# First network of a diffusion layer: 14 of 22 weight pairs as seven products of block sums, gated rows kept in DRAM

## Chip, cores, metric

One NeuronCore of one Trainium2 chip runs one launch of the kernel. The metric is device time in microseconds (us), the median over runs. The engines are called PE (TensorE), DVE (VectorE), ACT (ScalarE), POOL (GpSimd) and SP (SyncE, which here only issues DMAs). Every operand is float32 or float32r.

## What is computed

One layer of a hybrid diffusion backbone, on 512 latent tokens and 256 context tokens of width 1024. The part that changes is the first half-step feed-forward network, which runs on both token kinds with the same weights and with modulation vectors of their own:

```python
def swiglu(u, w_up, w_down):
    a, b = jnp.split(u @ w_up, 2, axis=-1)
    return (jax.nn.silu(a) * b) @ w_down          # w_up 1024 x 5632, w_down 2816 x 1024

def ffn_sublayer(h, m, i, w_up, w_down):
    shift, scale, gate = sub_mod(m, i)            # three of nine vectors, silu(c) @ w_ada + b_ada
    y = swiglu(modulate(h, shift, scale), w_up, w_down)
    return post_ln(DEEPNORM_ALPHA * h + 0.5 * gate * y, ln_g[i], ln_b[i])

x = ffn_sublayer(x, mod_x, 0, ffn1_w_in, ffn1_w_out)
ctx = ffn_sublayer(ctx, mod_c, 0, ffn1_w_in, ffn1_w_out)
```

After it come the input projections, neighbourhood attention and gated DeltaNet, their merge, and a second feed-forward network on the latent tokens alone. These do not change.

## The kernel before

**Accuracy.** Every float32 operand of the large products is split in a high and a low half (`split`, lines 134 to 139: ACT casts to float32r, DVE subtracts), and each 128 x 128 block is multiplied three times: high x high, low tokens x high weights, high tokens x low weights (lines 192 to 194 for the up-projections, line 211 for the down-projections).

**Tiling.** The 5632 columns of `w_up` are 22 pairs of 128 gate and 128 value columns. One pair is two weight tiles of 128 x 1024 (eight blocks along the 1024 inputs). `ffn_unit` multiplies a pair with all 512 latent or all 256 context tokens into two PSUM banks, and `glu` gates the result (silu on ACT, product on DVE) and splits it into `hx` (latent) or `hc` (context).

**Order.** (1) Pairs 0 to 2 on latent tokens while the modulation of the tokens is still being made; pairs 3 to 7 on latent tokens, with the context's modulation between; then pairs 0 to 7 on context tokens, their weights loaded again. (2) `up_phase`: pairs 8 to 10, each on both kinds. (3) `down` for the first 11 rows of `w_down`: all four latent blocks of 128 tokens in eight PSUM banks, then both context blocks. The results are gated, added to the inputs and kept in SBUF as `accx` and `accc` (lines 481 and 482). (4) `up_phase` for pairs 11 to 21. (5) `down` for the other 11 rows, then normalisation (`finish1`), and transposing and splitting of the new tokens (`u2`).

**What runs beside it.** The other modulation vectors are made on DVE. `ada_gen` is a generator; each step loads one 128 x 1024 tile of the transposed `w_ada` and takes its dot product with one or two broadcast rows (`dot_cols`, line 281). There are 56 steps, the first 24 with two dots. `up_phase` takes four steps per pair.

**What sets the order.** Weights go through `Stream`: loads on the SP queue, a raw buffer, then the split, one tile ahead of use and limited by the buffers (two high/low buffers in `wp`, every third tile in the one of `wx`). Raw buffers for weights, modulation tiles and token rows come from one counter, `raw1()`, which goes round five buffers: two in `wp`, two in the pool `more[0]` and one in `wx`. The program is traced in the order of its text; the framework's scheduler then fixes each engine's and queue's order ahead of time by a timing model of its own, adds the semaphores and hands out buffers. At run time each queue keeps to that order.

The second network already runs most of its pairs as seven products (lines 1456 to 1521), with token halves of 256.

Of the kernel before, what the change touches and what calls it, by code (L numbers as in the profile page):

```python
# [18 lines left out]
P = 128  # L19
# [39 lines left out]
def body(ctx, tc, I, out, dbg=None):  # L59
# [223 lines left out]
    def load_crow(tp):  # L283
        r = tl(tp, [P, 2, D], "crow")
        nc.scalar.dma_start(r[0:1], I["c_row"])
        return r

# [8 lines left out]
    def ada_gen(tp, wp, crow):  # L296
        for sec in range(2, 9):
            which = [(0, colx)] + ([(1, colc)] if sec < 5 else [])
            sl = slice(sec * 8, sec * 8 + 8)
            for k in range(KT):  # L300
                raw = raw1()
                nc.sync.dma_start(raw[:], I["w_adaT"][sec * KT + k])
                for w, col in which:
                    dot_cols(tp, raw, crow[:, w], col, sec * 8 + k)
                if k < KT - 1:
                    yield
            for w, col in which:
# [12 lines left out]
    raws, more = [0], [None]  # L320
# [6 lines left out]
    ap_, close_ap = pool("acc1")  # L327
    hcp, close_hcp = pool("hc1")
    up, close_up = pool("u1")

    uxh = tl(up, [P, KT, NX], "uxh", 1, F32R)
    uxl = tl(up, [P, KT, NX], "uxl", 1, F32R)

    tl(up, [P, 16], "gap")
    uch = tl(up, [P, KT, NCT], "uch", 1, F32R)
    ucl = tl(up, [P, KT, NCT], "ucl", 1, F32R)
    tl(up, [P, 48], "gap2")
# [7 lines left out]
    hxp, close_hxp = pool("hx1", "right")  # L345
    tp, close_tp = pool("t1")
    more[0] = tp
    xn = {"x": [], "c": []}

    def modulate_k(pp, kind, k):  # L350

        w, col, uh, ul, n = (0, colx, uxh, uxl, NX) if kind == "x" else (1, colc, uch, ucl, NCT)
# [4 lines left out]
        for sec in range(2):  # L357
            c0 = sec * 8 + k
            V.scalar_tensor_tensor(col[:, c0:c0 + 1], col[:, c0:c0 + 1], float(sec), bcol[:, c0:c0 + 1], op0=ALU.add, op1=ALU.add)
# [3 lines left out]
        u32 = tl(tp, [P, NX], "fs", 2)  # L363
        S.activation(u32[:, 0:n], ps[:], AF.Identity, bias=col[:, k:k + 1], scale=col[:, 8 + k:9 + k])
        split(u32[:, 0:n], uh[:, k], ul[:, k])

    def order1():
        t = lambda fs: [I["up1"][2 * f + j] for f in fs for j in range(2)]
        dn = lambda a, b: rows(I["dn1"], range(a, b))
        o = t(range(F0, F1)) + t(range(F1)) + t(range(F1, HF)) + dn(0, HF) + dn(0, HF - 2)  # L370
        o += t(range(HF, NF)) + dn(HF, NF - 4)
        n = len(o)
        o += dn(HF, NF - KL1)
        o = [(w, "x") if j % 3 == 2 else w for j, w in enumerate(o)]
        return o[:n] + [(w, "tail") for w in dn(NF - 4, NF)] + o[n:]

    def h_x():
        h = tl(hxp, [P, 2, NX], "hx", HF, F32R)
        return h[:, 0], h[:, 1]

    def h_c():
        h = tl(hcp, [P, 2, NCT], "hc", HF, F32R)
# [3 lines left out]
    F0, F1, KC, KL1, KL2 = 3, 8, 2, 6, 6  # L386
    PSB = [2]
    pp0, close_pp0 = pool("pp0", space=PSUM)
    crow = load_crow(tp)
    for t in range(4):  # L390
        x_t = tl(ap_, [P, D], f"ax{t}")
        (nc.scalar if t % 2 else nc.sync).dma_start(x_t[:], tok_src("x", t))
# [3 lines left out]
    for x_t in xn["x"]:  # L396
        ln_norm(tp, x_t[:], x_t, act=True)
    nc.sync.dma_start(bcol[:], I["b_col"])
    w0, acc0 = [], []

    def start_f(f):
        for j in range(2):
            raw = tl(ap_, [P, D], f"ac{j}")
            nc.sync.dma_start(raw[:], I["up1"][2 * f + j])
            if 2 * f + j < 3:
                hi, lo = [(tl(wp, [P, D], n, WB, F32R) if 2 * f + j < 2 else tl(wx, [P, D], n, 1, F32R))[:] for n in ("wh", "wl")]
            else:
                hi, lo = [tl(hxp, [P, 2, NX], "hx", HF, F32R)[:].rearrange("p a n -> p (a n)") for _ in range(2)]
            split(raw[:], hi, lo)
# [27 lines left out]
    for t in range(2):  # L437
        raw = raw1()
        nc.sync.dma_start(raw[:], tok_src("c", t))
        xn["c"].append(tl(ap_, [P, D], f"ac{t}"))  # L440
# [1264 lines left out]
```

## Time and profile before

| | us |
|---|---|
| median of 3 runs | 1522.52 (1520.34 to 1522.91) |
| profiled execution, whole time | 1518.13 |
| its span | 1516.4 |
| PE busy | 1458.7 (96%) |
| DVE busy | 1047.0 (69%) |
| ACT busy | 607.6 (40%) |
| POOL busy | 196.4 (13%) |

The first network fills roughly the first 580 us of the span. Its stages, in us from the start of the span: latent part of pairs 0 to 7 until 119.6, context part of these pairs until 165.0, pairs 8 to 10 until 214.6, first down stage until 303.6, pairs 11 to 21 until 486.0, second down stage until about 579.5. "Busy" is the time in which an instruction runs. Matmuls are pipelined, so the distance between the starts of two of them, and not the duration in a row, is what one costs. In a row of a timeline the first number is the start, the second the duration; in a group of instructions the numbers behind the bar are the sum of busy time and the mean in ns, then the idle time before them and what ended it.

### The profile page before, as it was taken

The page shows a single profiled execution, that of the slowest core. Times are in us where ns is not written, and L with a number is a line of the kernel's source. Part 1 is how long each engine was busy: PE and PEld are TensorE (multiplying, and loading weights), DVE is VectorE, ACT ScalarE, POOL GpSimd, SP SyncE. Part 2 cuts the span into 40 slices and gives each one's busy share as a digit, 9 for nine tenths or more (in the row PEclk, how much of TensorE's full clock was granted, in tenths as well). Part 3 has the DMA queues.
Part 4 walks back from the last instruction along what each step waited for, and adds up shares of the span by engine and source line. Part 5 has one row for each costly group of instructions (what it writes and reads, how often), then busy time and mean ns, then how long its engine had stood idle before and what let it go on. Part 6 is the DMA issues. An engine that isn't in the chain of part 4 may idle for free.

```text
span 1516.4 us, 23760 instructions
## 1 busy us (share of the span) xinstructions
PE 1458.7 (96%) x9286; PEld 1259.4 (83%) x9286; DVE 1047.0 (69%) x1792; ACT 607.6 (40%) x1009; POOL 196.4 (13%) x225
## 2 busy tenths in 40 slices
PE   6999999999999999999996899999999999999997
PEld 4789988888888888889874788867778999998886
DVE  8765852597554487758777896567669699886326
ACT  5444321222222255655542444267516444444310
POOL 0000000000000011323301001243221022220001
PEclk9999999999999999999998999999999999999999
DMA  9665642667554424222476634274343143233322
GB/s 369 204 237 188 221 145 97 206 206 253 196 179 139 142 111 142 96 83 89 139 212 178 172 97 132 78 255 151 97 171 141 57 139 111 98 112 141 137 84 84
DMA packets 107587, 230.73 MB, mean 152 GB/s; under 512 B 34177, under 2 KB 47825, under 8 KB 107473
## 3 DMA queue, kind: packets, MB, share of 16 engines
q1 hardware_dynamic: 105312, 221.79, 43.5%
q10 hardware_dynamic: 1586, 5.32, 0.9%
q0 software_dynamic: 576, 2.10, 0.4%
q8 instruction: 73, 1.20, 0.3%
q14 instruction: 40, 0.33, 0.1%
HBM read 206.33 MB, written 22.85 MB: 151 GB/s over the span
## 4 chain that ended last, share of the span: by engine, by line
PE 81%; DVE 9%; DMA 5%; issue 2%; ACT 1%; POOL 1%; SPq 1%; DVEq 0%; POOLq 0%; ACTq 0%
PE ps L211 22%; PE ps L192 9%; PE ps L194 9%; PE ps L193 8%; PE pm L192 5%; PE pm L194 5%; PE pm L193 5%; PE pc L862 3%; PE ps L1492 2%; PE ps L1493 2%; PE ps L1494 2%; DVE wl L139 2%; PE po L1272 1%; DMA Dt<-gcd 1%; PE pt L1261 1%
## 5 line engine op out<-in xcount | busy, mean ns | idle before, releaser
L139 DVE TENSOR_TENSOR wl<-wr,wh 128x1024 fp32r<-128x1024 f32 (+1 forms) x215 | 263.2, 1228 | 190.3 <-ACT wh L137 189.4
L137 ACT CAST wh<-wr 128x1024 fp32r<-128x1024 f32 (+1 forms) x215 | 217.9, 1018 | 325.0 <-PE ps L211 100.8
L194 PE MATMUL ps<-uxh,wl 128*128 128x512 f32 (+1 forms) x496 | 179.7, 364 | 0.5 <-DVE wl L139 0.5
L192 PE MATMUL ps<-uxh,wh 128*128 128x512 f32 (+1 forms) x496 | 180.0, 366 | 0.0
L193 PE MATMUL ps<-uxl,wh 128*128 128x512 f32 (+1 forms) x496 | 179.5, 363 | 0.0
L281 DVE SCALAR_TENSOR_TENSOR adap<-wr,crow 128x1024 f32<-128x1024 f32 x112 | 136.8, 1222 | 39.0 <-DMA wr<-in_w_adaT_dram 37.6
L114 POOL TENSOR_TENSOR rs<-ve,mhalf 128x1 f32<-128x1 f32 (+2 forms) x46 | 50.6, 1103 | 743.4 <-DVE ve L110 740.5
L192 PE MATMUL pm<-uxh,wh 128*128 128x512 f32 x320 | 131.8, 412 | 0.8 <-ACT spill L611 0.8
L194 PE MATMUL pm<-uxh,wl 128*128 128x512 f32 x320 | 127.2, 398 | 0.7 <-DVE wl L139 0.7
L193 PE MATMUL pm<-uxl,wh 128*128 128x512 f32 x320 | 126.9, 397 | 0.0
L194 PEld LDWEIGHTS ps<-uxh,wl 128*128 128x128 f32 x496 | 93.9, 189 | 16.2 <-DVE wl L139 1.3
L192 PEld LDWEIGHTS ps<-uxh,wh 128*128 128x128 f32 x496 | 93.7, 190 | 14.6 <-issue 0.8
L193 PEld LDWEIGHTS ps<-uxl,wh 128*128 128x128 f32 x496 | 94.0, 189 | 13.9
L192 PE MATMUL ps<-uch,wh 128*128 128x256 f32 x352 | 98.6, 280 | 0.0
L194 PE MATMUL ps<-uch,wl 128*128 128x256 f32 x352 | 98.3, 279 | 0.0
L193 PE MATMUL ps<-ucl,wh 128*128 128x256 f32 x352 | 98.2, 279 | 0.0
L211 PE MATMUL ps<-wh,hx 128*128 128x512 f32 x352 | 94.8, 389 | 0.0
L211 PEld LDWEIGHTS ps<-wh,hx 128*128 128x128 f32 x352 | 65.9, 188 | 13.6
L194 PEld LDWEIGHTS pm<-uxh,wl 128*128 128x128 f32 x320 | 60.9, 190 | 14.4 <-DVE wl L139 1.5
L192 PEld LDWEIGHTS pm<-uxh,wh 128*128 128x128 f32 x320 | 61.0, 190 | 12.6 <-ACT spill L611 1.5
L193 PEld LDWEIGHTS pm<-uxl,wh 128*128 128x128 f32 x320 | 61.1, 191 | 10.3
L192 PEld LDWEIGHTS ps<-uch,wh 128*128 128x128 f32 x352 | 66.1, 188 | 0.6
(417 smaller groups left out, 3416.6 us busy)
## 6 DMA issues: line engine op xcount, KB each, us to landing
wr<-in_w_adaT_dram SPq DMA_DIRECT2D x88, 512.0 KB, 4.4
wr<-in_up_dram SPq DMA_DIRECT2D x80, 512.0 KB, 3.6
wr<-in_dn_dram SPq DMA_DIRECT2D x58, 512.0 KB, 3.5
wr<-in_win_dram SPq DMA_DIRECT2D x52, 512.0 KB, 3.7
rb<-in_up_dram SPq DMA_DIRECT2D x18, 512.0 KB, 3.5
wr<-in_w_o_dram SPq DMA_DIRECT2D x8, 512.0 KB, 4.4
ac<-in_up_dram SPq DMA_DIRECT2D x6, 512.0 KB, 4.9
Dt<-gcd SPq DMA_DIRECT2D x12, 256.0 KB, 4.8
```

The source lines that it names most:

```text
L114: G.tensor_tensor(rs[:], ve[:], mhalf[:, 0:n], ALU.pow)
L137: S.copy(hi, src)
L139: V.tensor_tensor(lo, src, hi.bitcast(F32), ALU.subtract)
L192: T.matmul(ps, a, uh[:, k, :], start=(k == 0), stop=False)
L193: T.matmul(ps, a, ul[:, k, :], start=False, stop=False)
L194: marks["mm"] = T.matmul(ps, b, uh[:, k, :], start=False, stop=(k == nk - 1)).ins
L211: T.matmul(banks[t][d][:, c0:c1], a[:, sl], b[:, d * 512 + c0:d * 512 + c1], start=first and j == 0, stop=last and j == 2)
L281: V.scalar_tensor_tensor(pr[:], raw[:], 1.0, crow, op0=ALU.mult, op1=ALU.mult, accum_out=col[:, c:c + 1])
L862: last[0] = T.matmul(*a, **k).ins
L1492: T.matmul(ps[:], a, uh[:, k], start=k == 0, stop=False)
L1493: T.matmul(ps[:], a, ul[:, k], start=False, stop=False)
L1494: T.matmul(ps[:], b, uh[:, k], start=False, stop=k == 3)
```

## The change

Pairs 0 to 7 stay as they are (with one modulation step per pair in the context part, three before it), and are followed at once by the first down stage over their 8 rows. Pairs 8 to 21 run as seven products per pair, over latent and context tokens together: 768 tokens in two halves of 384, the 1024 inputs in two halves of 512, the 256 output columns in gate and value. The block sums of the tokens are made once, in the first down stage (`sums`). The block sums of a pair's weights are made while the pair before runs (`r` in `run` is the next pair; `prep_a`, `prep_s`, `prep_3`, `prep_b`). ACT copies two products out of PSUM, DVE adds the other five to them, and the gated rows of a pair (128 x 768) are written to DRAM (`hd`) by a DMA on the POOL queue. The second down stage has 14 rows, reads the gated rows back and splits them then (`h_load`). The accumulators of the first down stage go through DRAM as well (`accd`). The modulation steps move: 17 up to the end of the first down stage's latent part, 21 in the product loop, 18 in the latent part of the second down stage, where their tiles go through one buffer of the pool `l1`. The list of raw buffers in `raw1()` and the places of the first token tiles change too.

```diff
-                raw = raw1()
+                raw = raw_of[0]()
                 nc.sync.dma_start(raw[:], I["w_adaT"][sec * KT + k])
...
-        k = raws[0] % (5 if more[0] else 3)
-        return tl(more[0], [P, D], "wr", 2) if k > 2 else tl(wx, [P, D], "wr") if k == 0 else tl(wp, [P, D], "wr", WB)
+        k = raws[0] % 5
+        return tl(tp, [P, D], "wr") if k == 0 else tl(tp, [P, D], "ra", 2) if k > 2 else tl(wp, [P, D], "wr", WB)
...
+    N1 = 8
+    N2 = NF - N1
+    CX = 384
+    L0, L1, K0, K1 = slice(0, CX), slice(CX, 2 * CX), slice(0, 4), slice(4, 8)
+    uh = tl(up, [P, KT, 2 * CX], "uh", 1, F32R)
+    ul = tl(up, [P, KT, 2 * CX], "ul", 1, F32R)
+    row_tile = lambda dt: tl(up, [P, 2, CX], "ur", 14, dt)
+    ur = dict((k, row_tile(F32)) for j in range(4) for k in (j, j + 4))
+    uxh, uxl = uh[:, :, 0:NX], ul[:, :, 0:NX]
+    uch, ucl = uh[:, :, NX:], ul[:, :, NX:]
...
-    F0, F1, KC, KL1, KL2 = 3, 8, 2, 6, 6
+    F0, KC, KL1, KL2 = 3, 2, 5, 6
+    ADA2 = [1] * 7 + [2] * 7
+    ADA3 = [2] * 9
...
+    def sums(k):
+        a, b, c, d = ur[k][:, 0], ur[k][:, 1], ur[k + 4][:, 0], ur[k + 4][:, 1]
+        for o, i0, i1 in ((a, b, a), (b, d, b), (d, d, a), (c, c, d)):
+            V.tensor_tensor(o, i0, i1, ALU.subtract)
+        split(b, uh[:, k, L1], ul[:, k, L1])
+        for i, t in ((5, a), (6, d), (4, c)):
+            trow[i, k] = r = row_tile(F32R)
+            split(t, r[:, 0], r[:, 1])
...
+    def t_sums(j):
+        if j < 4:
+            sums(j)
+        ada_step()
...
-        banks, tail = down(pp, ws, hs, n, 2 if kind == "x" else 0, tail if kind == "c" else ())
+        banks, tail = down(pp, ws, hs, n, 2 if kind == "x" else 0, tail if kind == "c" else (), between=t_sums if kind == "x" else None)
         for t in range(n):
             xr = raw1()
             nc.sync.dma_start(xr[:], tok_src(kind, t))
+            tmp = tl(tp, [P, D], "adap")
             for d in range(2):
                 sl = slice(d * 512, (d + 1) * 512)
-                V.tensor_tensor(acc[t][:, sl], banks[t][d][:], g[:, sl], ALU.mult)
-                V.scalar_tensor_tensor(acc[t][:, sl], xr[:, sl], ALPHA, acc[t][:, sl], op0=ALU.mult, op1=ALU.add)
+                V.tensor_tensor(tmp[:, sl], banks[t][d][:], g[d][:], ALU.mult)
+                V.scalar_tensor_tensor(xr[:, sl], xr[:, sl], ALPHA, tmp[:, sl], op0=ALU.mult, op1=ALU.add)
+            nc.gpsimd.dma_start(accd[t + 4 * (kind == "c")], xr[:])
...
+    class Seven:
+        def __init__(self, f):
+            self.f, self.w = f, {}
+            self.ra, self.rb = tl(tp, [P, D], "ra", 2), tl(wp, [P, D], "wr", WB)
+            nc.sync.dma_start(self.ra[:], I["up1"][2 * f])
+            nc.sync.dma_start(self.rb[:], I["up1"][2 * f + 1])
...
+        def prep_a(self):
+            self.keep(self.ra[:], tl(wx, [P, D], "wh", 1, F32R)[:], tl(wx, [P, D], "wl", 1, F32R)[:], (1, 2))
+        def prep_s(self):
+            s, rb = sraw[0], self.rb
+            V.tensor_tensor(s[:, 0:512], rb[:, 0:512], rb[:, 512:], ALU.add)
+            V.tensor_tensor(s[:, 512:D], s[:, 0:512], self.ra[:, 0:512], ALU.subtract)
+            self.keep(s[:, 0:D], tl(wp, [P, D], "wh", WB, F32R)[:], tl(wp, [P, D], "wl", WB, F32R)[:], (5, 6))
+        def prep_3(self):
+            s = sraw[0]
+            V.tensor_tensor(s[:, D:], self.ra[:, 512:], s[:, 512:D], ALU.subtract)
+            self.keep(s[:, D:], tl(tp, [P, 512], "fs", 2, F32R)[:], tl(tp, [P, 512], "fs", 2, F32R)[:], (3,))
+        def prep_b(self):
+            ra, rb = self.ra, self.rb
+            V.tensor_tensor(rb[:, 0:512], ra[:, 0:512], rb[:, 0:512], ALU.subtract)
+            self.keep(rb[:], tl(wp, [P, D], "wh", WB, F32R)[:], tl(wp, [P, D], "wl", WB, F32R)[:], (7, 4))
+        def product(self, i):
+            ps = tl(pp, [P, CX], "ps", 8)
+            wh, wl = self.w[i]
+            for k, (mh, ml) in enumerate(moved[i]):
+                a, b = wh[:, k * P:(k + 1) * P], wl[:, k * P:(k + 1) * P]
+                T.matmul(ps[:], a, mh, start=k == 0, stop=False)
+                T.matmul(ps[:], a, ml, start=False, stop=False)
+                T.matmul(ps[:], b, mh, start=False, stop=k == 3)
+            return ps[:]
+        def run(self, r):
+            c1, c2 = parts[self.f % 2]
+            c11, c12, c21, c22 = c1[:, 0], c1[:, 1], c2[:, 0], c2[:, 1]
+            p = self.product(1)
+            S.copy(c11, p)
+            p2 = self.product(2)
+            if r:
+                r.prep_a()
+            p5 = self.product(5)
+            S.copy(c22, p5)
+            V.tensor_tensor(c21, c11, self.product(6), ALU.add)
+            V.tensor_tensor(c11, c11, p2, ALU.add)
+            V.tensor_tensor(c12, c21, c22, ALU.add)
+            if r:
+                r.prep_s()
+            V.tensor_tensor(c12, c12, self.product(3), ALU.add)
+            S.activation(c1[:], c1[:], AF.Silu)
+            if r:
+                r.prep_3()
+            V.tensor_tensor(c21, c21, self.product(7), ALU.add)
+            V.tensor_tensor(c22, c21, c22, ALU.add)
+            V.tensor_tensor(c21, c21, self.product(4), ALU.add)
+            V.tensor_tensor(c1[:], c1[:], c2[:], ALU.mult)
+            nc.gpsimd.dma_start(hd[self.f - N1].rearrange("p (a n) -> p a n", a=2), c1[:])
+            if r:
+                r.prep_b()
...
+    fs = [Seven(N1), Seven(N1 + 1)]
+    fs[0].prep_a()
...
+    for f in range(N2):
+        fs[f].run(fs[f + 1] if f + 1 < N2 else None)
+        if f + 2 < N2:
+            fs.append(Seven(N1 + f + 2))
+        ada_step(ADA2[f])
...
+    ada_raw[0] = lambda: tl(lp, [P, D], "wr")
...
+    def h_load(t, src):
+        nc.sync.dma_start(t[:, 1].bitcast(F32), src)
+        split(t[:, 1].bitcast(F32), t[:, 0], t[:, 1])
+        return t[:, 0], t[:, 1]
...
+    def h_next(j):
+        h_split(j + 6)
+        h_split_c(2 * j + 2)
+        ada_step(ADA3[j])
+
+    h_split(4)
+    bx, tail = down(pp, ws, hx, 4, KL1, between=h_next, n=N2)
...
-    FIN1, AFC = (0, 2, 5, 9), (0, 3)
-    down(pp, ws, hc, 2, 0, tail[:-4], between, after, post=tail[-4:])
+    FIN1 = (0, 2, 5, 8)
+    down(pp, ws, hc, 2, 0, tail[:-NT], between, after, post=tail[-NT:], n=N2)
```

More of the change, by code (lines that the diff above doesn't have):

```diff
@@ L294, in spread_crow, with ada_gen @@
             S.activation(r[:, w, d * 512:(d + 1) * 512], ps[d][:], AF.Silu)
-    def ada_gen(tp, wp, crow):
+    def ada_gen(tps, raw_of, crow):
         for sec in range(2, 9):
@@ L343, in tok_src @@
         return I["x" if kind == "x" else "ctx"][t * P:(t + 1) * P, :]
-    hxp, close_hxp = pool("hx1", "right")
-    tp, close_tp = pool("t1")
-    more[0] = tp
     xn = {"x": [], "c": []}
     def modulate_k(pp, kind, k):
-        w, col, uh, ul, n = (0, colx, uxh, uxl, NX) if kind == "x" else (1, colc, uch, ucl, NCT)
+        w, col, c0, n = (0, colx, 0, NX) if kind == "x" else (1, colc, NX, NCT)
         for sec in range(2):
@@ L407, in start_f @@
             else:
-                hi, lo = [tl(hxp, [P, 2, NX], "hx", HF, F32R)[:].rearrange("p a n -> p (a n)") for _ in range(2)]
-            split(raw[:], hi, lo)
+                hi, lo = [tl(hxp, [P, 2, NX], "hx", N1, F32R)[:].rearrange("p a n -> p (a n)") for _ in range(2)]
+            split(raw, hi, lo)
             w0.append((hi, lo))
@@ L439, in body, with ada_step, rows_out @@
         nc.sync.dma_start(raw[:], tok_src("c", t))
-        xn["c"].append(tl(ap_, [P, D], f"ac{t}"))
-        ln_norm(tp, xn["c"][t][:], raw, act=True)
-    for f in range(F0, F1):
+        xn["c"].append(tl(st0, [P, D], f"x{t}")[:])
+        ln_norm(tp, xn["c"][t], raw, act=True)
+    gates = {k: tl(dp, [8, P], "gate")[:] for k in ((0, 2), (1, 2), (0, 5), (0, 8))}
+    ada_tp, ada_raw, rows_due = [tp], [raw1], []
+    ada = ada_gen(ada_tp, ada_raw, crow)
+    def ada_step(n=1):
+        for _ in range(n):
+            next(ada, None)
+    def rows_out(pp):
+        while rows_due:
+            w, sec = rows_due.pop(0)
+            to_row(ada_tp[0], pp, secs((colx, colc)[w], sec), gates[(w, sec)])
+    for f in range(F0, N1):
         hx.append(h_x())
@@ L489, in body @@
+    close_sg()
     close_tp()
     close_up()
+    accp, close_accp = pool("acc1")
+    accx = [tl(accp, [P, D], f"ax{t}") for t in range(4)]
+    for t in range(4):
+        nc.gpsimd.dma_start(accx[t][:], accd[t])
+    hcp, close_hcp = pool("hc1")
     lp, close_lp = pool("l1")
+    ada_tp[0] = lp
+    ada_raw[0] = lambda: tl(lp, [P, D], "wr")
     gx = tl(lp, [P, D], "g")
@@ L536, in body @@
     x1c = [tl(fc, [P, D], f"x1c{t}") for t in range(2)]
+    for t in range(2):
+        nc.gpsimd.dma_start(x1c[t][:], accd[4 + t])
     def between(j):
```

160 lines of the change are left out of this document (88 added, 72 removed).

## The prediction

> **What bounds the kernel now.** I read the page from the top (busy shares, then the chain), then the windows by stage, then single matmuls for their spacing.
>
> ```profile
> span 1516.4 us, 23760 instructions
> PE 1458.7 (96%) x9286; PEld 1259.4 (83%) x9286; DVE 1047.0 (69%) x1792; ACT 607.6 (40%) x1009; POOL 196.4 (13%) x225
> PE 81%; DVE 9%; DMA 5%; issue 2%; ACT 1%; POOL 1%; SPq 1%; DVEq 0%; POOLq 0%; ACTq 0%
> GB/s 369 204 237 188 221 145 97 206 206 253 196 179 139 142 111 142 96 83 89 139 212 178 172 97 132 78 255 151 97 171 141 57 139 111 98 112 141 137 84 84
> ```
>
> TensorE (PE) is busy for 96% and carries the chain. The windows (columns: length, then busy time of PE, weight load, DVE, ACT, POOL; clock; DMA share; GB/s) say what that means in the first network:
>
> ```profile
> 119.60:165.00 45.40, 45.40 (x383) 45.22 (x382) 28.88 (x39) 21.88 (x33) 0.00 (x0) 1.00 0.53 187
> 214.60:274.00 59.40, 59.40 (x264) 49.18 (x263) 20.28 (x24) 10.16 (x11) 0.00 (x0) 1.00 0.33 114
> 303.60:486.00 182.40, 182.40 (x1059) 161.40 (x1059) 120.47 (x192) 43.34 (x66) 0.00 (x0) 1.00 0.57 191
> 1225.00:1305.00 80.00, 80.00 (x659) 78.03 (x658) 76.67 (x107) 37.47 (x54) 21.41 (x15) 1.00 0.33 113
> ```
>
> The rows are: context half of pairs 0 to 7; latent down-projection; up-projection of pairs 11 to 21; and, last, the second network's own seven-product loop. PE never pauses and its clock is 1.00, so these stages last what their matmuls last. Matmuls removed shorten the span one for one, as long as nothing new makes PE wait.
>
> **The change, part by part.** *Matmuls of 14 pairs.* The spacing of starts (first and last of six latent, 25 context and 55 second-network matmuls):
>
> ```profile
> 329.73 0.39 PE L192 MATMUL ps<-uxh,wh 128*128 128x512 f32 x1
> 330.86 0.39 PE L194 MATMUL ps<-uxh,wl 128*128 128x512 f32 x1
> 331.09 0.28 PE L192 MATMUL ps<-uch,wh 128*128 128x256 f32 x1
> 333.92 0.28 PE L192 MATMUL ps<-uch,wh 128*128 128x256 f32 x1
> 1240.08 0.28 PE L1492 MATMUL ps<-t14h,sh 128*128 128x256 f32 x1
> 1246.20 0.28 PE L1492 MATMUL ps<-t14h,bh 128*128 128x256 f32 x1
> ```
>
> That is 0.226, 0.118 and 0.1133 us: 0.442 ns per column for 512 wide and for the 256 wide of the products, 0.461 for the context's. A pair costs 2 x 8 x 3 = 48 latent and 48 context matmuls, 48 x (0.2267 + 0.118) = 16.5 us. The silu activations agree, 165.88 us for ten pairs and 33.92 for six context pairs:
>
> ```profile
> 128.23 0.38 ACT L273 ACTIVATE fs<-ps 128x256 f32<-128x256 f32 x1
> 162.15 0.38 ACT L273 ACTIVATE fs<-ps 128x256 f32<-128x256 f32 x1
> 309.28 0.60 ACT L273 ACTIVATE fs<-ps 128x512 f32<-128x512 f32 x1 [4.38 <-PE ps L194]
> 475.16 0.60 ACT L273 ACTIVATE fs<-ps 128x512 f32<-128x512 f32 x1 [4.30 <-PE ps L194]
> ```
>
> so 16.59 and 5.65 us. Seven products are 7 x 4 x 3 = 84 matmuls of 384 columns; none is in the trace, and between 0.442 and 0.461 ns per column it is 0.170 to 0.177 us. I take 0.170, since 512 and 256 wide agree on it: 14.28 us a pair. Term: 14 x (14.28 - 16.59) = -32.3 us (-24 at the dear end). The down-projections keep all their matmuls, only cut 8 and 14 instead of 11 and 11.
>
> *VectorE (DVE) in the product loop.* Rows:
>
> ```profile
> L281 DVE SCALAR_TENSOR_TENSOR adap<-wr,crow 128x1024 f32<-128x1024 f32 x96 | 117.3, 1222 | 38.9 <-DMA wr<-in_w_adaT_dram 37.6 <-ACT crow L294 0.3
> L139 DVE TENSOR_TENSOR wl<-wr,wh 128x1024 fp32r<-128x1024 f32 x96 | 117.2, 1223 | 112.2 <-ACT wh L137 111.6
> L139 DVE TENSOR_TENSOR hx<-fs,hx 128x512 fp32r<-128x512 f32 x22 | 15.1, 689 | 5.6 <-ACT hx L137 5.5
> L139 DVE TENSOR_TENSOR hc<-fs,hc 128x256 fp32r<-128x256 f32 x22 | 9.2, 419 | 0.0
> L281 DVE DVE_READ_ACCUMULATOR adap<-wr,crow 128x1 f32 x96 | 7.9, 82 | 0.0
> L137 ACT CAST wh<-wr 128x1024 fp32r<-128x1024 f32 x175 | 183.1, 1050 | 259.9 <-PE ps L211 70.2 <-PE ps L193 58.1 <-PE pm L193 52.2
> 1240.81 0.41 DVE L1514 TENSOR_TENSOR sn<-sn,ps 128x256 f32<-128x256 f32 x1
> 1241.14 0.41 DVE L1515 TENSOR_TENSOR sn<-sn 128x256 f32<-128x256 f32 x1
> ```
>
> Per pair: low halves 3 x 1.22 + 0.69; four 512-wide weight sums at 0.69; seven 384-wide product sums at 0.55 (between 0.42 and 0.69); one 768-wide product at 0.96; two modulation dots at 1.30 (ADA2 gives one step of two dots, later two steps of one). Sum 14.6 us busy, but starts lie 0.33 apart where an instruction shows 0.41, so some 0.08 each is overlap and 19 instructions need about 13.0 of the 14.28 us. The second network's window ran DVE 76.67 of 80 us with PE full, so I charge 2 us for 14 pairs (bounds 0, and 1 us a pair = 14). ScalarE needs half of that time. The GpSimd queue carries the gated rows out and nobody waits for them until the second down stage.
>
> *Context half of pairs 0 to 7* gets one modulation step each: DVE 2 x 1.22 + 2 x 0.42 + 2 x 1.30 = 5.9 us busy, about 5.4 without overlap, against 5.65; three 0.52 MB loads per 5.65 us are 278 GB/s, above the 187 there but below the first slice's 369. Weights are two ahead. Charge 1 us (0 to 5).
>
> *First down stage.* Block sums of the tokens: eight 384-wide operations per step, 8 x 0.55 + 2.6 (dots) + 1.22 (weight) = 8.2 us against 24 x 0.2267 = 5.44 of PE, for four steps: 11 us behind, about the two weights held ahead. Charge 2 us (0 to 8). Each accumulator now sits in a raw buffer until it has been written to DRAM, and context weights wait for those buffers: 1 us (0 to 4).
>
> *The step into the product loop.* Counting `raw1()` calls, the two context rows are the 96th and 97th, both in `wp`'s "wr", the two buffers in which `Seven` loads its second weight tile. What the chain costs:
>
> ```profile
> 303.35 1.88 DVE L481 TENSOR_TENSOR ac<-ps,g 128x512 f32<-128x512 f32 x3
> wr<-in_w_adaT_dram SPq DMA_DIRECT2D x88, 512.0 KB, 4.4
> wr<-in_up_dram SPq DMA_DIRECT2D x80, 512.0 KB, 3.6
> xr<-x1d POOLq DMA_DIRECT2D x4, 512.0 KB, 6.2
> ```
>
> Four evacuation operations from 0.3 us before the last context matmul (303.35 against 303.64): 4 x 0.69 puts them 2.4 us behind it; a GpSimd-queue transfer 6.2, load 3.6, two sums 1.4, cast 1.05, low half 1.22: 15.9 us. Until then PE has products 1 and 2 (24 x 0.170 = 4.1 us), and, if the order takes those of the next pair forward, 4.1 more. Wait 7.7 to 11.8; zero if the order avoids it. I take 9, near the middle of the two. The Trainium skill (DMA: Bandwidth & Descriptors, "Anatomy of one DMA — SWDGE (gpsimd) path") puts such a transfer at 2.0 us plus bytes over 436 GB/s, which is 3.2 us for 512 KB, estimated from that page; this trace's row says 6.2. By the page the sum below would be 3 us lower.
>
> A wait of this length has an after-effect, seen in the trace's longest PE wait:
>
> ```profile
> 827.12 0.69 PE L862 MATMUL pi<-T,Bt 32*32 32x32 f32 x32 [14.87 <-DMA T<-rd]
> 829.19 0.63 PE L192 MATMUL pm<-uxh,wh 128*128 128x512 f32 x1
> 829.61 0.63 PE L193 MATMUL pm<-uxl,wh 128*128 128x512 f32 x1
> 831.75 0.39 PE L194 MATMUL pm<-uxh,wl 128*128 128x512 f32 x1
> 831.98 0.40 PE L192 MATMUL pm<-uxh,wh 128*128 128x512 f32 x1
> 824.00:828.00 4.00, 0.88 (x33) 0.82 (x34) 1.93 (x12) 0.82 (x3) 0.64 (x4) 0.50 0.87 216
> 828.00:832.00 4.00, 4.00 (x42) 2.77 (x43) 3.76 (x14) 2.33 (x4) 3.44 (x7) 0.60 0.22 66
> ```
>
> After it the granted clock is 0.50 and matmuls stand 0.42 us apart until about 831.2, then 0.23: some 3.5 us at half rate, 1.7 us lost. Charge 1.7. The Trainium skill (TensorE: Matmul & The Clock Gate, Part 1) states the same, half clock after an idle window of about 3.4 us; this row agrees with it.
>
> *The step out of the product loop.* The second down weight needs the buffer of the last product's weights: cast 1.05 and low half 1.22 after it, covered by the first weight's 5.44 us. If that cover is gone, 2.3 us. Charge 1 (0 to 5).
>
> *Second down stage.* Per weight of 5.44 us it now loads a weight, two modulation rows, one latent and two context gated tiles: 2.1 MB, 385 GB/s against 369 as the best slice. All 18 modulation steps go through one buffer in `lp`: load 4.4 + dot 1.30 = 5.7 us each, 103 us in all, against 14 x 5.44 = 76 us of this stage and 38 of the context part. They need not be done earlier, but they sit in SP's and DVE's order with the weights. Charge 4 us (0 to 54, rival B).
>
> The context part then has more weights to cover the same normalisations; nothing is charged. The start is the same work in other buffers.
>
> **Sum.** -32.3 + 2 + 1 + 2 + 1 + 9 + 1.7 + 1 + 4 = -10.6 us. The profiled execution took 1518.13 us (1.7 around its span), 4.4 below the median of 1522.52. Against the median: 1511.9, forecast 1512.
>
> **Rivals.**
> A, *the waits are hidden*: the order fills the step into the loop, and the second down stage keeps up. For it: PE waits nowhere in the first network after its start. Then -32.3 plus 1 or 2: 1491 to 1493.
>
> B, *the single modulation buffer starves the second down stage; slower*. If SP keeps two modulation loads ahead of each weight load, a weight comes every 2 x 5.7 = 11.4 us instead of 5.44: nine times 6 us = +54. With the other terms (-14.6) the time is 1562; a third of it gives 1526. It decides from 14.6 / 9 = 1.6 us of wait per weight. For it is the row of waits,
>
> ```profile
> DVE adap L281 <- DMA wr<-in_w_adaT_dram: 37.6, 27, 4.0
> ```
>
> where dots reach DVE's head before their data, 27 times, up to 4.0 us, with five buffers; against it, that PE did not wait then, and that the steps may be ordered late, into the context part.
>
> C, *DVE becomes the bound of the loop*: at 16 us a pair instead of 14.28, 24 us more, less the 2 charged: 1534; at 15 us, 1520. Against it is the second network's window.
>
> **How the numbers follow.** Chances: forecast 0.47, A 0.18, B 0.25, C 0.10. What a measurement tells from no change is 0.2%, 3 us. Faster: forecast, A, half of C, a little of B (0.02): 0.72. Slower: most of B (0.19) and 0.02 of C: 0.21. Same: 0.07. The range runs from A's 1491 to 1535, which leaves out B's dear half, about one in ten, and little else; the forecast's own range is 1502 to 1520.
>
> **What would show it.** Right: 84 matmuls of 384 columns a pair, 0.170 us apart, 14.3 us between their silus; one PE wait of 8 to 12 us shortly before the first product 5, then a clock of 0.5 for some 3 us; DVE above 85% in the loop with PE full. Wrong: spacing of 0.177 or more; PE waiting in the loop for DVE; PE waits in the second down stage for weight low halves (DVE) behind dots that wait for a DMA; no wait at the step into the loop.

## The result and the profile after

The change makes the kernel slower. The changed kernel takes 1561.81 us (median of 4 runs, 1556.16 to 1562.79), against 1522.17 for the kernel before (4 runs, 1520.34 to 1522.91): a ratio of 1.0255, 95% interval 1.0228 to 1.0281. The forecast was 1512, in a range of 1491 to 1535. The profiled execution took 1556.16 us and has a span of 1554.4; it lies 5.7 us below the median, and that of the kernel before 4.0 below its own, so the two profiles can be set against each other to within 2 us.

The page of the changed kernel, the same rows as were shown of the kernel before (span, busy shares, shares of the chain):

```profile
span 1554.4 us, 23869 instructions
PE 1441.8 (93%) x9118; PEld 1261.2 (81%) x9118; DVE 1160.5 (75%) x1993; ACT 650.2 (42%) x1068; POOL 212.5 (14%) x251
PE 59%; DVE 18%; DMA 13%; issue 5%; ACT 3%; POOL 2%; SPq 1%; DVEq 0%; ACTq 0%; POOLq 0%
```

PE has 16.9 us less to do, DVE 113 us more, and PE's share of the chain fell from 81% to 59%, with DVE and DMA in its place. The waits of PE say where:

```profile
PE ps L242 <- DVE colx L303: 33.4, 1, 33.4
...
PE ps L555 <- ACT wh L137: 9.1, 1, 9.1
```

Both are single waits and both are new. The windows of the changed kernel's first network (length, then busy time of PE, weight load, DVE, ACT, POOL; clock; DMA share; GB/s):

```profile
117.82:172.07 54.25, 49.22 (x387) 48.12 (x386) 50.37 (x83) 25.27 (x40) 0.00 (x0) 0.94 0.71 234
172.07:217.54 45.47, 43.94 (x195) 35.90 (x193) 34.64 (x56) 10.55 (x16) 0.73 (x1) 1.00 0.64 211
217.54:243.32 25.78, 23.26 (x98) 17.58 (x96) 12.82 (x16) 6.20 (x6) 1.60 (x3) 1.00 0.85 292
262.00:340.00 78.00, 78.00 (x451) 78.00 (x450) 78.00 (x127) 30.50 (x41) 2.17 (x4) 1.00 0.60 205
400.00:458.80 58.80, 58.80 (x340) 58.80 (x339) 39.38 (x58) 20.64 (x26) 3.52 (x7) 1.00 0.24 83
458.84:538.88 80.04, 77.93 (x337) 62.50 (x337) 49.00 (x75) 22.14 (x33) 3.84 (x6) 1.00 0.77 273
538.88:572.56 33.68, 0.30 (x3) 0.03 (x2) 30.36 (x60) 2.67 (x3) 6.70 (x7) 0.57 0.49 171
572.56:577.00 4.44, 4.44 (x12) 3.48 (x13) 0.00 (x0) 0.34 (x2) 0.00 (x0) 0.50 0.03 7
```

In order: context half of pairs 0 to 7; first down stage, latent and context; the product loop near its begin and near its end; second down stage, latent; a stretch of 33.68 us in which PE does three matmuls; the first context matmuls after it, at half clock. By stages, each from the start of its first matmul. For the kernel before these starts are 118.66 (context half), 163.89 (pairs 8 to 10), 213.84, 303.64, 486.02 and 579.55; the stage times given above for the first three lie some 1 us behind them:

| stage | before | after | difference |
|---|---|---|---|
| context half of pairs 0 to 7 | 45.2 | 54.3 | +9.0 |
| the other 14 pairs | 232.3 | 215.5 | -16.8 |
| first and second down stage together (22 rows) | 183.3 | 229.3 | +46.0 |
| end of the first network | 579.5 | 616.9 | +37.4 |
| from there to the end of the span | 936.9 | 937.5 | +0.6 |

The context half starts 0.8 us earlier than before (117.82), which closes the sum. So most of the loss is in the down stages, and the larger part of it is one wait. PE's timeline there:

```profile
538.43 0.61 PE L211 MATMUL ps<-wh,hx 128*128 128x512 f32 x2
538.88 0.27 PE L242 MATMUL ps<-ident,colx 128*8 128x128 f32 x1
572.53 0.37 PE L242 MATMUL ps<-ident,colx 128*8 128x128 f32 x1 [33.38 <-DVE colx L303]
572.56 1.20 PE L211 MATMUL ps<-wh,hc 128*128 128x512 f32 x2
```

Line 242 is `to_row`: a transpose of eight modulation columns, 0.27 us of work. The call `rows_out(pp)`, which transposes two gate vectors here, stands in the text behind the latent evacuations and ahead of the context part of `down`. So the two transposes stand on PE ahead of 14 rows of context matmuls, and the second of them needs the last of all modulation steps. DVE's timeline at the end of that chain, first and last of the last 15 dots in the second down stage:

```profile
497.63 1.22 DVE L281 SCALAR_TENSOR_TENSOR adap<-wr,crow 128x1024 f32<-128x1024 f32 x1 [2.65 <-DMA wr<-in_w_adaT_dram]
...
571.05 1.22 DVE L281 SCALAR_TENSOR_TENSOR adap<-wr,crow 128x1024 f32<-128x1024 f32 x1 [1.30 <-DMA wr<-in_w_adaT_dram]
572.20 0.08 DVE L281 DVE_READ_ACCUMULATOR adap<-wr,crow 128x1 f32 x1
572.31 0.17 DVE L303 SCALAR_TENSOR_TENSOR colx<-colx,bcol 128x8 f32<-128x8 f32 x1
```

Fourteen steps in 73.42 us are 5.24 us each, the round trip of the one buffer, and the last ends 33.4 us behind the latent part. Of the 18 dots that were meant to run beside the latent part 11 start in it. The trace of the kernel before had the figure against which this could have been read; the rows of the tile `colx` (duration least, median, most; first and last start) of the kernel before, then of the changed one:

```profile
L308 DVE SCALAR_TENSOR_TENSOR colx<-colx,bcol x7: 158/159/168, 187.4 to 473.7; 128x8 f32<-128x8 f32 x7
L242 PE MATMUL ps<-ident,colx x3: 270/270/270, 197.0 to 486.0; 128*8 128x128 f32 x3
```

```profile
L303 DVE SCALAR_TENSOR_TENSOR colx<-colx,bcol x7: 157/161/166, 158.6 to 572.3; 128x8 f32<-128x8 f32 x7
L242 PE MATMUL ps<-ident,colx x3: 270/271/373, 166.7 to 572.5; 128*8 128x128 f32 x3
```

Before, the last vector was complete at 473.7 and its transposes done at 486.0, ahead of the second down stage. The change moved the last 18 steps into that stage and left the transposes between its two halves.

### The profile page after: what moved, and what is told of

It is laid out like the page before. It is cut to its first block, busy times and chain, and to the rows that moved or that the text cites. A ratio compares the mean times of both kernels' runs of the same rounds, so it can differ in the third digit from the quotient of the medians.

```text
span 1554.4 us, 23869 instructions
## 1 busy us (share of the span) xinstructions
PE 1441.8 (93%) x9118; PEld 1261.2 (81%) x9118; DVE 1160.5 (75%) x1993; ACT 650.2 (42%) x1068; POOL 212.5 (14%) x251
## 4 chain that ended last, share of the span: by engine, by line
PE 59%; DVE 18%; DMA 13%; issue 5%; ACT 3%; POOL 2%; SPq 1%; DVEq 0%; ACTq 0%; POOLq 0%
PE ps L211 10%; PE ps L555 4%; PE pm L192 4%; PE ps L556 4%; PE ps L557 4%; PE pm L194 4%; PE pm L193 4%; DVE wl L139 3%; DMA wr<-in_dn_dram 3%; PE ps L193 3%; PE pc L1018 3%; PE ps L192 3%; PE ps L194 3%; DVE adap L281 2%; PE ps L1650 2%
## 5 line engine op out<-in xcount | busy, mean ns | idle before, releaser
L139 DVE TENSOR_TENSOR wl<-wr,wh 128x1024 fp32r<-128x1024 f32 (+1 forms) x186 | 230.7, 1244 | 118.3 <-ACT wh L137 118.1
L281 DVE SCALAR_TENSOR_TENSOR adap<-wr,crow 128x1024 f32<-128x1024 f32 x86 | 104.9, 1220 | 16.8 <-DMA wr<-in_w_adaT_dram 16.1
L192 PE MATMUL ps<-uh,wh 128*128 128x256 f32 (+1 forms) x208 | 69.0, 332 | 1.6 <-ACT wh L137 1.6
L194 PE MATMUL ps<-uh,wl 128*128 128x256 f32 (+1 forms) x208 | 68.2, 330 | 2.3 <-DVE wl L139 2.3
L193 PE MATMUL ps<-ul,wh 128*128 128x256 f32 (+1 forms) x208 | 68.3, 328 | 2.0 <-DVE ul L139 2.0
L555 PE MATMUL ps<-ur,wh 128*128 128x384 f32 x168 | 57.2, 341 | 9.1 <-ACT wh L137 9.1
L193 PE MATMUL ps<-uxl,wh 128*128 128x256 f32 (+1 forms) x192 | 60.5, 317 | 0.9 <-DVE uxl L139 0.9
L194 PE MATMUL ps<-uxh,wl 128*128 128x256 f32 (+1 forms) x192 | 60.3, 317 | 0.0
L192 PE MATMUL ps<-uxh,wh 128*128 128x256 f32 (+1 forms) x192 | 59.7, 317 | 0.0
L211 PE MATMUL ps<-wl,hx 128*128 128x512 f32 x176 | 55.4, 391 | 1.7 <-DVE wl L139 1.7
L556 PE MATMUL ps<-ur,wh 128*128 128x384 f32 x168 | 57.0, 339 | 0.0
L555 PE MATMUL ps<-uh,wh 128*128 128x384 f32 x168 | 56.6, 337 | 0.0
```

Of the source, the lines that this page charges most:

```text
L139: V.tensor_tensor(lo, src, hi.bitcast(F32), ALU.subtract)
L192: T.matmul(ps, a, uh[:, k, :], start=(k == 0), stop=False)
L193: T.matmul(ps, a, ul[:, k, :], start=False, stop=False)
L194: marks["mm"] = T.matmul(ps, b, uh[:, k, :], start=False, stop=(k == nk - 1)).ins
L211: T.matmul(banks[t][d][:, c0:c1], a[:, sl], b[:, d * 512 + c0:d * 512 + c1], start=first and j == 0, stop=last and j == 2)
L281: V.scalar_tensor_tensor(pr[:], raw[:], 1.0, crow, op0=ALU.mult, op1=ALU.mult, accum_out=col[:, c:c + 1])
```

## The experiments

Theory S: the single buffer in `lp` makes the modulation chain end late, the transposes stand in PE's order ahead of ready work, and both together are the loss. Theory D: behind that wait DVE is nearly full (30.36 of 33.68 us), so that PE would wait for weights if it did not wait for the transpose. For the smaller losses the theories are named at the runs. The ratios below are to runs of the kernel before that were made beside each group of experiments (medians between 1519.7 and 1523.1).

**1. The transposes behind the context part.**

```diff
-    rows_out(pp)
     gc = tl(lp, [P, D], "g")
     ...
     down(pp, ws, hc, 2, 0, tail[:-NT], between, after, post=tail[-NT:], n=N2)
+    rows_out(pp)
```

> The two transposes that turn modulation columns into gate rows (line 242) are issued behind the context part of the second down stage instead of ahead of it; nothing else moves in the text. Theory S (a transpose that needs the last modulation step stands ahead of the context part in PE's order, and the steps come 5.2 us apart through one buffer): the wait of 33.4 us and the slow clock after it (1.7 us) go, about 35 us faster than the changed kernel, 1527 us. Rival D (DVE, busy for 30.4 of the 33.7 us of that wait, is the limit, so its evacuations and normalisations hold PE anyway): the context part starts at once but waits for weight halves or normalised rows, and less than 15 us is won, 1547 us or more.

Measured: 1552.35 us, ratio to before 1.0183 (1.0157 to 1.0208). The wait at line 242 is gone and 9.5 us are won, where S alone expected 35. The windows of the second down stage in this run, latent and context part:

```profile
461.75:544.19 82.44, 77.71 (x337) 62.61 (x337) 48.72 (x75) 22.21 (x33) 3.84 (x6) 1.00 0.79 266
544.19:600.00 55.81, 45.19 (x203) 35.60 (x201) 52.12 (x88) 31.49 (x57) 7.83 (x7) 0.95 0.62 201
```

The context part now starts at once, but DVE is busy for 52.12 of 55.81 us, with the modulation dots, the evacuations, the normalisations and the low halves of weights in one queue, and PE waits for low halves in four places:

```profile
PE ps L211 <- DVE wl L139: 6.3, 4, 2.5
```

The stage lasts 138.3 us instead of 158.1. At the pace of the kernel before it would be 118: 93.5 us for 11 rows, and 8.2 for each of three more. So D is right as to the size: taking the transposes out of the way does not help the work that piles up behind the late chain. Of the 19.8 us won in this stage 9.5 are left in the medians: the stage starts 2.9 us later, and the work behind the first network takes 15.8 us longer in this profile (more on this below). It begins with the clock at 0.50 for 3 us, after a wait of 4.2 us for the new tokens.

**2. Two buffers for the chain.**

```diff
-    ada_raw[0] = lambda: tl(lp, [P, D], "wr")
+    ada_raw[0] = lambda: tl(lp, [P, D], "wr", 2)
```

> The modulation tiles of the second down stage get two buffers in place of one; the transposes stay ahead of the context part. Theory S: steps come about 3 us apart while the latent part runs, the last of 18 is done by 520 us or so instead of 572, the wait of 33.4 us goes or shrinks below 5, about 1527 to 1532 us. Rival D: the steps follow DVE and not the buffer, the spacing stays near 5 us and the time within 10 us of 1562.

Measured: 1534.62 us, ratio 1.0075 (1.0059 to 1.0091): 27 us less than the change. The windows of the second down stage here:

```profile
459.41:540.00 80.59, 76.81 (x337) 62.81 (x337) 56.59 (x89) 22.30 (x33) 3.24 (x6) 1.00 0.88 310
540.00:587.20 47.20, 43.86 (x204) 34.61 (x203) 41.73 (x69) 30.54 (x57) 9.57 (x8) 1.00 0.52 170
```

The last dot, and the two transposes:

```profile
535.75 1.22 DVE L281 SCALAR_TENSOR_TENSOR adap<-wr,crow 128x1024 f32<-128x1024 f32 x1
540.00 0.38 PE L242 MATMUL ps<-ident,colx 128*8 128x128 f32 x2
```

Against the changed kernel, 7.6 us of DVE work moved from behind the latent part into it, where DVE had been idle for 31 us (80.04 - 49.00); the last dot starts at 535.75 instead of 571.05, and the transposes run at 540.00 without a wait. The latent part got no longer for it (80.6 against 80.0) although DMA moved 310 instead of 273 GB/s. Theory S had expected more, the last step by 520 us and 1527 to 1532 in all: the 18 dots start 3.9 us apart in the mean and not 3. With run 1 this settles the main cause: the round trip of one buffer set when the chain ended, and the place of the transposes handed that to PE.

**3. The context's old tokens in tiles that are free.** In the changed kernel the two context rows of the first down stage take `wp`'s two "wr" buffers, and `Seven` loads into the same two. Here they take gate tiles that nobody needs any more:

```diff
-            xr = raw1()
-            nc.sync.dma_start(xr[:], tok_src(kind, t))
+            xr = raw1()[:] if kind == "x" else tl(hxp, [P, 2, NX], "hx", N1, F32R)[:].rearrange("p a n -> p (a n)").bitcast(F32)
+            nc.sync.dma_start(xr, tok_src(kind, t))
```

> The two context rows of the first down stage are loaded into free latent gate tiles, not into the two buffers that the first pairs' second weight tiles need. If those buffers hold up the step into the product loop: the wait of 9.1 us before the first sum product and the slow clock after it (granted 0.71 to 0.73 around it) go, 9 to 11 us faster, about 1551 us. Rival: the first sums wait for DVE (14.3 of 14.7 us busy there) or for the context gate, and the wait stays above 5 us.

Measured: 1549.23 us, ratio 1.0172 (1.0156 to 1.0188): 12.6 us less than the change. The window that held the wait is full:

```profile
247.00:262.00 15.00, 15.00 (x89) 15.00 (x88) 14.71 (x24) 6.24 (x9) 1.06 (x2) 1.00 0.54 179
```

The loop lasts 205.8 us instead of 215.5, which is 14 pairs at 14.70. So the step into the loop costs 9.7 us, by those two buffers.

**4. The context half of pairs 0 to 7, dots made small.** This part is 9 us longer than before. Two theories: DVE's time for the dots, or the third load per pair. The context's dots of the first 11 steps run on 64 of the 1024 columns; the rest of these sums is left out.

```diff
-        V.scalar_tensor_tensor(pr[:], raw[:], 1.0, crow, ..., accum_out=col[:, c:c + 1])
+        V.scalar_tensor_tensor(pr[:, 0:n], raw[:, 0:n], 1.0, crow[:, 0:n], ..., accum_out=col[:, c:c + 1])
...
-                    dot_cols(tps[0], raw, crow[:, w], col, sec * 8 + k)
+                    dot_cols(tps[0], raw, crow[:, w], col, sec * 8 + k, 64 if w and narrow[0] else D)
```

> The context dot products of the first eleven modulation steps take 64 of 1024 columns, which leaves out most of these sums; loads and order of the text stay. The context part of pairs 0 to 7 took 52.4 us against 45.2 before. If DVE's load makes that (48.5 of 52.4 us busy): the stage comes back to 45 to 47 us and the whole run is some 6 us shorter. Rival: the third 512 KB load per pair, or the raw buffers it holds, makes it, and the stage stays above 50 us.

Measured: one run, 1560.61 us. The part lasts 52.3 us, from 117.9 to 170.2, against 54.3 in the changed kernel, with DVE busy for 43.10 us instead of 50.37:

```profile
117.90:170.20 52.30, 47.90 (x386) 46.37 (x385) 43.10 (x83) 25.75 (x41) 0.00 (x0) 0.97 0.69 242
```

The part gets 2 us shorter for 7.3 us less work on DVE: the dots' time alone is not what makes it long.

**5. The block sums held back.** In the changed kernel the framework's scheduler took the block sums of the tokens forward into this part. Here they wait for the last context gate:

```diff
-            sums(j)
+            with tc.issue_after(gated_by[0]):
+                sums(j)
```

> The token block sums of the first down stage are held on DVE behind the last context gate; in the changed kernel's trace most of them ran 15 to 60 us earlier, inside the latent and context part of pairs 0 to 7, where DVE then had no idle time. If they are what lengthens that part (narrow dots did not shorten it): the context part takes 45 to 48 us instead of 52.4, its PE waits of 0.8 to 2.0 us go, and the first down stage gives back at most 3 us: 3 to 6 us faster than the changed kernel. Rival: the third load per pair does it, the part stays above 50 us and the first down stage grows by 5 us or more, so the run is no faster.

Measured: 1562.97 us, ratio 1.0285 (1.0261 to 1.031), no gain. The part lasts 55.7 us, 1.5 longer than in the changed kernel. DVE and PE in it:

```profile
128.18 1.23 DVE L281 SCALAR_TENSOR_TENSOR adap<-ra,crow 128x1024 f32<-128x1024 f32 x1 [4.17 <-DMA ra<-in_w_adaT_dram]
129.33 0.08 DVE L281 DVE_READ_ACCUMULATOR adap<-ra,crow 128x1 f32 x1
129.33 1.22 DVE L139 TENSOR_TENSOR wl<-wr,wh 128x1024 fp32r<-128x1024 f32 x1
```

```profile
130.60 0.58 PE L194 MATMUL ps<-uh,wl 128*128 128x256 f32 x1 [4.05 <-DVE wl L139]
```

Without the sums DVE reaches a modulation dot before its data, waits for 4.17 us, and the low half that stands behind the dot makes PE wait for 4.05.

**6 and 7. The three edits together, then with the transposes moved as well.** Edits 2, 3 and 5; then also edit 1.

> Two modulation buffers in the second down stage, context rows in gate tiles, and the block sums held back, together. If the three costs are separate: 1562 - 27 - 12.5 - 5 = 1517 us, some 0.3% faster than before the change. If they overlap (time won ahead of the second down stage is lost there to DVE): 1522 to 1527, no faster than before.

> As the three edits together, and the gate-row transposes behind the context part as well. With two buffers the steps are done when the latent part ends, so by the theory of the single buffer nothing is left to win: within 3 us of the three edits. If PE still waited on DVE's modulation work there, it would be 5 us or more faster.

Measured: 1531.45 us, ratio 1.0071 (1.0052 to 1.0091), and 1529.68, ratio 1.0061 (1.0042 to 1.0081). Both expectations of the sixth run were missed, the sum of the three gains (1517) by 14 us and the overlap (1522 to 1527) by 4. As expected of the seventh, the place of the transposes no longer matters once the chain ends in time.

**8. Edits 2 and 3 alone.** The edits are those shown above.

> The second modulation buffer and the gate tiles for the context's old tokens, without the held block sums. The second buffer alone gave 1534.6 us and the gate tiles alone took 12.6 us off. Theory A (the two act on different stages and the held sums cost what the three together lacked): 1522 to 1525 us, the product loop at about 206 us and the second down stage at about 128. Rival (what is won in the first network is partly given back by the later stages, whose order is planned anew, and the held sums cost nothing): 1530 to 1533 us, as with all three, with the end of the first network near 578 us.

Measured: 1518.59 us (12 runs) against 1522.41 (23 runs), ratio 0.998 (0.9967 to 0.9993): the fastest version that leaves nothing out, about 0.2% below the kernel before. Better than theory A by 3 us, and the rival fell: the hold of edit 5 had cost all that the three together lacked, 4 us of it in the first network (which ends at 578.2 us here and at 582.3 in run 6), the rest behind it. Even here little of the change is left: the 14 pairs take 26.5 us less than before (205.8), but the context half takes 8.5 more, the first down stage 6.3 and the second 10.8 more than as many rows took before, so that the first network ends only 1.4 us earlier. PE's row of the transposes in this run, both in one go:

```profile
529.66 0.38 PE L242 MATMUL ps<-ident,colx 128*8 128x128 f32 x2
```

**9. The eight loads of the context part left out.** On top of edits 2 and 3 the eight dots there run on a tile that is resident (`crow[:, 0]`, scaled by 0.001), and their loads are not made:

```diff
-                raw = raw_of[0]()
-                nc.sync.dma_start(raw[:], I["w_adaT"][sec * KT + k])
+                raw, by = crow[:, 0], 1e-3
+                if not 3 <= (sec - 2) * KT + k < 11:
+                    by = 1.0
+                    raw = raw_of[0]()
+                    nc.sync.dma_start(raw[:], I["w_adaT"][sec * KT + k])
```

> On top of the two edits, the eight modulation steps in the context part of pairs 0 to 7 do their dots on a tile that is resident, and their eight loads are left out (those sums of the modulation are left out with them). Theory A (the third load per pair, in the queue and the raw buffers of the weights, makes that part longer): the part falls from 52 us to 45 to 47, and the short PE waits at its begin go. Rival (the dots' time on DVE, which is busy for 49 of its 52 us, makes it): the part stays at 51 to 53 us.

Measured: one run, 1510.36 us, 8 us below run 8 on the same chip. The product loop starts at 237.06 instead of 243.53, so 6.5 us of it are here. But the part itself is only 1.5 us shorter than in run 8 (53.7), and most of the gain is in the first down stage, which lasts 66.9 us instead of 71.6:

```profile
117.97:170.15 52.18, 48.52 (x390) 47.72 (x389) 51.39 (x85) 25.69 (x40) 0.00 (x0) 0.97 0.60 190
```

DVE fills it to 98%, and the waits at its begin, which theory A had go, are still there (2.09 and 1.45 us). So the loads cost some 6 us over this part and the first down stage behind it, and the part itself went as the rival had it. That DVE is then its limit is read from this share and was not tested.

**10. Three modulation steps later**, in the product loop, on top of edits 2 and 3:

```diff
-    ADA2 = [1] * 7 + [2] * 7
+    ADA2 = [1] * 4 + [2] * 10
...
-        ada_step()
+        ada_step(f > 2)
```

> On top of the two edits, the modulation steps start with the fourth context pair, and the three that are left out there are taken in the product loop (two per pair from the fifth pair on, not from the eighth). Theory A (load and dots crowd the first pairs of the context part): the part falls from 52 to 47 to 49 us, the product loop stays at 206, and the kernel gains 3 to 5 us on the run with the two edits. Rival (DVE bound over the whole part and the first down stage): the part gains its three steps' 7 us of DVE, but the work waits behind it and the kernel stays within 1.5 us of the two edits.

Measured: 1527.08 us, ratio 1.0024 (1.0009 to 1.0039), slower than run 8, which neither expected. The context part did not get shorter (53.5 us), since the two first waits of PE in it are there as before: 2.03 and 1.45 us behind the low halves of tokens and weights, with the block sums ahead of these on DVE.

**11. Loads left out and sums held.** Edits 2, 3, 5 and 9; leaves out what run 9 leaves out.

> The run without the eight context loads, with the block sums held behind the last context gate as well (the same eight sums of the modulation are left out). Theory B (the context part has two limits of nearly one height: DVE, full from 104 us on with the block sums among the dots, and the wait for the third load per pair; each alone came to nothing or little, since the other is next): with both taken away the short waits near 121 and 124 us go and the part falls from 52 us (49 to 52 without the loads) to 45 to 47. Rival (its length is the products' own at the clock it has there, and the sums were never late for it): it stays at 49 to 52.

**12. Steps later and sums held.** Edits 2, 3, 5 and 10; nothing left out.

> The run with three modulation steps taken later, with the block sums held behind the last context gate: the first three context pairs then have neither sums nor modulation loads beside them, and nothing is left out. Theory B: the context part falls from 53 us to 47 to 49, and the kernel comes to 1519 to 1523 us, 4 to 8 below the run without the hold. Rival (the held sums fill the first down stage, where DVE is busy for 31 of 45 us, and the step into the products waits longer): the part is shorter, the first down stage and the step give it back, and the kernel stays at 1525 to 1529.

Measured: 1523.54 us (one run) and 1525.19 us, ratio 1.0038 (1.0022 to 1.0054). The windows of the context part, run 11 and run 12:

```profile
119.73:169.61 49.88, 46.03 (x387) 45.50 (x386) 45.59 (x71) 22.14 (x35) 0.00 (x0) 1.00 0.58 190
```

```profile
118.94:168.18 49.24, 46.91 (x388) 45.58 (x386) 37.44 (x58) 21.56 (x34) 0.00 (x0) 1.00 0.67 226
```

The clock is 1.00, and the part falls to 49 to 50 us, as the rival of run 11 and the upper end for run 12 had it, 4 to 5 us above the 45.2 before. In run 11 3.8 us of this are two PE waits (1.53 and 2.32) for low halves of weights that stand behind dots on DVE; in run 12 waits for casts and low halves are 2.3 us, and the rest was not followed up. From the first context matmul to the first product both runs need 122.8 us, against 125.3 in run 8 and 119.1 in run 9. The time of run 12 lies in its rival's range, but not for the rival's reason: the first down stage gives back hardly anything against run 10 (73.6 us against 73.1), the first network ends 5.0 us earlier than there and 1.4 earlier than in run 8, and what is lost against run 8 lies behind it (last section). Run 11 is 13 us slower than run 9, 5.1 in the first network and 8.1 behind it. So the 9 us have several parts on one DVE queue (dots, their late data, block sums, and half clock after the waits), and shifting one of them moves the wait; no run took all of it away.

## Why the prediction was wrong, by its own steps

| term | forecast, us | measured, us | from |
|---|---|---|---|
| matmuls of 14 pairs | -32.3 | -27.9 | silus 14.60 apart |
| DVE in the loop | +2 | 0 | windows, PE full |
| step into the loop, with half clock | +10.7 | +10.9 | wait 9.1, and 1.8 |
| context half of pairs 0 to 7 | +1 | +9.0 | stage table |
| first down stage, accumulators | +3 | +5.9 | 71.2 against 8/11 of 89.8 |
| step out, second down stage | +5 | +40 | 158.1 against 118 |
| sum | -10.6 | +37.9 | the first network's end moved by 37.4, its context half began 0.8 earlier |

**The step that failed** is the second down stage: "They need not be done earlier, but they sit in SP's and DVE's order with the weights. Charge 4 us (0 to 54, rival B)." The first half of this sentence was wrong. The prediction had the chain right (18 steps in one buffer, 5.7 us each, 103 us against a latent part of 76; measured 5.24 between dots and 80) and so had in its hand that it ends behind the latent part. It then looked only for those who share a queue with the chain, not for those who wait for its last result: two transposes, in PE's order ahead of the whole context part. The latent part, where the charge was laid, lasts 80.0 us against 76.4 for 14 rows, 3.6 more. The 33.7 at line 242 and some 2.5 behind it were nowhere in the sum.

**Rival B** gave 1562 and the median is 1561.8, but that is chance: its mechanism was weight loads held behind modulation loads, nine times 6 us in the latent part, with its mark in PE waits for low halves. In the latent part PE is idle for only 2.1 of 80.0 us. What B had right is the resource, the single buffer, which run 2 confirms. The point held against it, that the steps may be ordered late, is what happened.

**Matmul spacing**: no row was 384 wide, and the cheap end was taken. The changed kernel's timeline, first and last of nine starts:

```profile
440.05 0.34 PE L555 MATMUL ps<-uh,wh 128*128 128x384 f32 x1
...
441.44 0.34 PE L557 MATMUL ps<-uh,wl 128*128 128x384 f32 x1
```

1.39 us over eight are 0.174 us, 0.452 ns per column, between the two ends given (0.442 and 0.461). Over 84 matmuls this is 14.6 us, and the silus agree, two pairs apart:

```profile
412.22 0.85 ACT L576 ACTIVATE ur<-ur 128x768 f32<-128x768 f32 x1 [0.68 <-DVE ur L575]
...
441.42 0.85 ACT L576 ACTIVATE ur<-ur 128x768 f32<-128x768 f32 x1 [0.68 <-DVE ur L575]
```

14 x (29.20 / 2 - 16.59) = -27.9: the middle of the two ends would have been right.

**DVE in the loop**: right that it does not bind. It is full near the loop's begin (78.00 of 78.00, modulation dots taken forward) and two thirds busy near its end, and PE is full in both. Rival C fell.

**The step into the loop**: right in mechanism, place and size. The first product 5 starts after the one long wait of the loop, and the clock is halved behind it:

```profile
256.75 0.69 PE L555 MATMUL ps<-ur,wh 128*128 128x384 f32 x1 [9.11 <-ACT wh L137]
...
260.31 0.37 PE L555 MATMUL ps<-uh,wh 128*128 128x384 f32 x1
```

Between these rows the starts stand 0.32 us apart where they had been 0.174: 3.56 us at half rate, of which half, 1.8, is lost. In the sum of the wait one part was too dear: the two rows' way to DRAM, priced at 6.2 us. The estimate by the Trainium skill's formula for such a transfer (DMA: Bandwidth & Descriptors, "Anatomy of one DMA — SWDGE (gpsimd) path") is 3.2. Here the trace agrees with the page rather than with the row that was used, 3.3 as the median of the four writes out of "wr", among them those of the two rows (two others, out of "ra", took 5.6):

```profile
accd<-wr POOLq DMA_DIRECT2D x4, 512.0 KB, 3.3
```

That the 9 was met so closely is in part luck. From the last context matmul to the first product 5 it took 13.4 us (243.32 to 256.75) and not 15.9, and products covered 4.3 us of it, where the 9 stood near the middle of the cases with 4.1 and 8.2.

**The first down stage** had the right mechanism at half its size: in its context part PE waits 2.4 us for casts of weights that were loaded late, and SP waits up to 5.4 us for an accumulator's way to DRAM before it can load one.

**The context half** was mis-sized: DVE was counted at 5.4 us of 5.65 per pair, and the block sums were charged to the first down stage. The scheduler took them forward. DVE is full in the window around the begin of this part, and the first low halves come late:

```profile
104.00:130.00 26.00, 21.67 (x107) 18.34 (x106) 26.00 (x48) 12.83 (x23) 0.00 (x0) 0.88 0.56 183
```

The measured 9 us lie above the end of the range that was given (5).

## What to carry to other kernels

When a serial chain is moved later, work out when its last result comes, then find the first instruction that needs it on every in-order queue, however small that instruction is, and price everything that stands behind it there. A small late need (here 0.27 us of transposes) ahead of ready work costs the whole lateness of the chain; but moving it out of the way helps only as far as the engine that runs the chain has room behind it, and giving the chain a second buffer, so that it ends in a stage where that engine has idle time, was worth three times as much here. Tiles on which the first step of a new stage depends should not share buffers with the last step of the stage before.

## What the runs showed that was not expected

*Half clock after two short waits.* In the context part PE waits for 2.03 us, runs for 1 us, waits for 1.45, and is then at half clock:

```profile
122.39 0.39 PE L193 MATMUL ps<-ul,wh 128*128 128x256 f32 x1 [2.03 <-DVE ul L139]
...
124.93 0.58 PE L194 MATMUL ps<-uh,wl 128*128 128x256 f32 x1 [1.45 <-DVE wl L139]
```

```profile
122.00:125.00 3.00, 1.16 (x8) 0.96 (x8) 3.00 (x6) 1.01 (x1) 0.00 (x0) 0.80 0.00 0
125.00:130.00 5.00, 5.00 (x23) 5.00 (x24) 5.00 (x9) 2.39 (x5) 0.00 (x0) 0.50 0.67 220
```

The granted clock is 0.50 over the next 5 us, so some 2.5 us are lost on top of the 3.5 of waits. The Trainium skill (TensorE: Matmul & The Clock Gate, Part 1) ties the half clock to an idle window of about 3.4 us; here no single wait was that long. In run 8, with waits of 2.02 and 1.45, the clock was 0.51 for only 3 us, and in run 3, with 1.71 and 1.48, the mean clock of the part stayed at 1.00. Where the point lies, these runs do not say.

*The work behind the first network depends on what is done to the first network.* Its text is the same in all versions, but the order is planned anew from the whole program. The clean case is run 12 against run 8, whose profiled executions (1524.68 and 1518.61 us) both lie at their medians: the first network ends 1.4 us earlier in run 12 (576.8 against 578.2), and from there to the end of the span it takes 946.1 us instead of 938.6. It is 937.5 in the changed kernel, 937.3 in run 3 and 936.9 in the kernel before. Runs 8 and 12 ran on different chips, but the kernel before was faster, not slower, beside run 12 (1519.7 against 1522.41). So an edit can lose 7.5 us in work that it does not touch, twice what separates run 8 from the kernel before. Run 2 shows it too (943.6, in a profile 2.1 us below its median); runs 1, 6 and 10 show more of it (953.3, 949.6 and 946.5), but their profiled executions lie 2 to 3 us above their medians. In the traces of runs 8 and 12 DVE and ACT take the later work in different orders, so the order is the likely cause; that it is, and which step of it costs the time, was not tried.
